# Convolutions, gate operands and gate diagonals issued earlier in a bidirectional hybrid layer

## The chip, the core and the metric

One Trainium2 chip, one of its cores. The metric is the device time of one execution in microseconds. The core has TensorE (PE in the profile, with its weight loads as PEld), VectorE (DVE), ScalarE (ACT), GpSimd (POOL) and SyncE (SP, which issues DMAs).

## The reference, cut to what matters

One layer on a sequence of 2048 tokens with 2048 channels, in float32:

```
mod = silu(c) @ w_ada + b_ada;  shift, scale, gate = split(mod)
h = rms_norm(x) * (1 + scale) + shift
u_pool, u_lru, g_pool, g_lru = split(h @ w_in + b_in)
y_pool = pool_mixer(u_pool)                  # centred means of 2, 4, 8, 16 tokens, then a 256x256 product
v = depthwise_conv(u_lru, width 4)
for both directions:
    r, i = sigmoid(v @ w_gate + b_gate)
    a = exp(-8 r softplus(-lambda));  b = sqrt(1 - a^2) * i * v
    h_dir = scan(h = a h + b)
y_lru = h_forward + h_backward
y = concat(rms_norm(y_pool) * silu(g_pool), rms_norm(y_lru) * silu(g_lru)) @ w_out + b_out
out = rms_norm(x + gate * y)
```

## The kernel before, in words

Every product in float32 is done as three matmuls over operands split into a high and a low part (`mm3`): high by high, high by low, low by high. The program is one loop over 352 steps `t`. A step is 24 matmuls of 128x512 that add one slice of the contraction to four banks of PSUM. Steps 0 to 127 make the plain part of the input projection, steps 128 to 239 the rest of it with seven products in place of eight, steps 240 to 351 the output projection in the same way. Each step needs a tile `m` (activations, split in L184 on ScalarE and L185 on VectorE, three buffers) and a tile `s` (weights). When the last slice of a bank is added, it is evacuated: in steps 128 to 239 by `in_evac` (L494 to L513), some on ScalarE, most on VectorE.

The mixers run beside that as background work. `at(t, fn)` appends a function to the list `bg[t]`, which is called at the end of step t, in the order of the list. An LRU unit is one head, one direction `d` and one block of 512 tokens, and starts at a step `b` (tables `L_AT`; mostly five steps apart). Its parts are: for the forward direction a depthwise convolution in place on `u` (L560 on ScalarE, then L562 three times on VectorE, for each of two channel tiles, accumulating in `cv`); `split`, which makes the gate operand `uch` in its two parts (L567 on ScalarE, L568 on VectorE); `gates`, two groups of 12 matmuls for each of two channel tiles; `sig` (L581, L583); `expo`, tanh and exponential (L589, L593); `scan`, which begins with a square root on ScalarE (L597), then products (L602, L603) and the scan itself (L608 forward, L612 backward). There is one buffer for `uch` and one for the gate weights `gw` (L537, L538). The first four units of each head run forward, the other four backward and are merged with them (L630 to L635).

Late in the program (steps 257 to 259) `gate_rows` makes the row vector of the adaLN gate: it builds diagonal matrices from columns (L771) in a buffer of the pool `raw`, and a float32 matmul with ones (L774) turns them into rows; L775 evacuates them. Near that stands the norm of the last block: a matmul, a square root (L422) and a reciprocal (L423).

A scheduler decides the order of the instructions on each engine: it goes by the order in which the program issues them as priority, and by its own estimate of when operands are there. So a function issued earlier gets a higher priority than what follows, on every engine it uses. On the chip each engine runs its list in that order. Buffers come from pools: `raw` has eight buffers for loads, evacuated gates, scan results and diagonals, `ps_m` six banks of PSUM and `px` two.

Of the kernel before, what the change touches and what calls it, by code (L numbers as in the profile page):

```python
# [11 lines left out]
ALU = mybir.AluOpType  # L12
# [33 lines left out]
def layer(ctx: ExitStack, tc: tile.TileContext, xc, xn, c, wada, win, wgate, wpool, wout, vecs, consts, bout, fng, out):  # L46
    nc = tc.nc
# [15 lines left out]
    def raw(name):  # L63
        return raw_p.tile([128, 2, TB], F32, tag="raw", name=name)
# [7 lines left out]
    def pm():  # L72
        return ps_m.tile([128, TB], F32, tag="pm", name="pm")

    def px():
        return ps_x.tile([128, TB], F32, tag="px", name="px")
# [15 lines left out]
    cst = one.tile([128, NC], F32, name="cst")  # L92
    ones = one.tile([128, 128], F32, name="ones")
# [4 lines left out]
    gcol = one.tile([128, 16], F32, name="gcol")  # L98
# [20 lines left out]
    bg = defaultdict(list)  # L119

    def at(t, fn, *a):
        bg[t].append((fn, a))
# [6 lines left out]
    def where1(t):  # L129

        g, i = divmod(t, 32)
        if g == 0 and i < 16:
            return 0, i % 2, i // 2
        return g, i // 8, i % 8
# [7 lines left out]
    def where2(t):  # L142

        sg, i = divmod(t - T1, SG)
        return sg, i // 8, i // 4 % 2, i % 4
# [17 lines left out]
    def m_load(t):  # L163
        if t >= NT:
            return
        r = raw("xr")
        if t < T1:
            g, tb, p = where1(t)
            load(out=r, in_=xc[tb, p] if g < 2 else xscr[tb][p])
        else:  # L170
            sg, k, q, p = where2(t)
            load(out=r, in_=moving("in" if sg < 2 else "out", PRODUCTS[k][1], p, q))
        xraw[t] = r
# [43 lines left out]
    def w_load(g, p):  # L217
        r = raw("wr")
        load(out=r, in_=win[g, p])
        wraw[g, p] = r  # L220
# [120 lines left out]
    def step(bk, sk, p, m, tiles, first, last, by_j=False, more=False):  # L341

        s = S_t[sk, p]
        for n, j in [(n, j) for j in range(2) for n in tiles] if by_j else [(n, j) for n in tiles for j in range(2)]:
            mm3(bk[n], s, slice(n * 128, (n + 1) * 128), m, j, first and j == 0, last and j == 1, more)
# [53 lines left out]
    def ada_load(i):  # L399
        t = big("ada")[:, :D]  # L400
        load(out=t, in_=wada[i])
        ada_t[i] = t
# [143 lines left out]
    def lru_unit(g, h, d, tb, b, last):  # L546
# [91 lines left out]
                del u_t[g]  # L638

        if d == 0:  # L640
            at(b, conv)
        at(b, split)
        at(b + 2, gates, 0)
        at(b + 3, sig, 0)
        at(b + 3, gates, 1)
# [107 lines left out]
    def rows_open():  # L753
# [9 lines left out]
        for i, (tb, kind) in enumerate([(2, "P"), (2, "L"), (3, "P"), (3, "L")]):  # L763
            act(out=fin["rn"][:, i], in_=rn_t[tb, kind], func=AF.Copy)
            rn_t[tb, kind] = fin["rn"][:, i]

    def gate_rows(i):
        t = raw("dg")[:, 0]
        for j in range(4):
            k = 4 * i + j  # L770
            nc.vector.tensor_scalar(out=t[:, j * 128:(j + 1) * 128], in0=cst[:, 0:128], scalar1=gcol[:, k:k + 1], scalar2=None,  # L771
                                    op0=ALU.mult)
        ps = px()
        nc.tensor.matmul(out=ps, lhsT=ones, rhs=t, start=True, stop=True)  # L774
        act(out=fin["gate"][:, i * TB:(i + 1) * TB], in_=ps, func=AF.Copy)  # L775
        if i == 3:
            vtt(out=fin["gb"], in0=fin["gb"], in1=fin["gate"], op=ALU.mult)
# [95 lines left out]
    for i in range(16):  # L873
        b = 17 + i * 5 // 4
# [32 lines left out]
    for g, bs in L_AT.items():  # L907
        h = GROUPS[g][1]
        for d in range(2):
            b = bs[4 * d]  # L910
# [9 lines left out]
    for i in range(32):  # L920
        p, k, q = i // 8, (0, 2, 1, 3)[i // 2 % 4], i % 2
# [4 lines left out]
    for sg in range(2):  # L926
        b = NT1 + SG * sg
# [47 lines left out]
    for t, tb, kind in rn_at:  # L975
        at(t, rn, tb, kind)
    at(256, rows_open)
    for i in range(4):
        at(257 + i * 3 // 4, gate_rows, i)


    unit_at = {T1 - 6 + 2 * u: u for u in range(112)}
# [10 lines left out]
    def s_step(p):  # L993
        ada_dot(16 + 2 * p)
        ada_dot(17 + 2 * p)
        scale_fin(p)
        w_split(0, p)
# [4 lines left out]
    for t in range(NT):  # L1002

        if t < 16:
            if t % 2 == 0:
                p = t // 2
                if p + 1 < 8:
                    w_load(0, p + 1)
                m_load(t + 2)
                m_load(t + 3)  # L1010
                if p + 2 < 8:
                    ada_load(16 + 2 * p + 4)
                    ada_load(16 + 2 * p + 5)
        if t >= 14:
            while loaded < t + AHEAD:
                loaded += 1
                m_load(loaded)
        if t < T1:
            g, tb, p = where1(t)
            key = (g, tb)  # L1020
            sk = g
            first, last = p == 0, p == 7
        else:
            sg, k, q, p = where2(t)
            more = k in CHAINED and (sg == 3 or sg == 2 and k == 6)
            key = (8 + sg, CHAINED[k] if more else k, q)
            sk = (8 + sg, PRODUCTS[k][0])
            first, last = p == 0 and not more, p == 3
        e = t + W_AHEAD - 25
        if 0 <= e < 96 and e % 32 < 8:  # L1030
            w_load(e // 32 + 1, e % 32)
        if t + W_AHEAD in unit_at:
            unit_load(unit_at[t + W_AHEAD])
        for o, i in late:
            store(out=o, in_=i)
        late.clear()

        if t < 14:
            if t % 2 == 0:
                s_step(t // 2 + 1)  # L1040
        if 32 <= t + 3 < 64:
            modulate(t + 3)
        m_split(t + 2)
        e = t - 25
        if 0 <= e < 96 and e % 32 < 8:
            w_split(e // 32 + 1, e % 32)
        if t in unit_at:
            unit_split(unit_at[t])

        if key not in banks:  # L1050
            if t == 0:
                banks[key] = [px(), px(), pm(), pm()]
            else:
                banks[key] = [px(), px(), pm(), pm()] if q and t >= T1 and (sg == 3 or sg == 2 and k > 1) else [pm() for _ in range(4)]
        bk = banks[key]
        if t < NT - 4:
            step(bk, sk, p, M_t.pop(t), range(4), first, last, t == 0, t >= T1 and more)
        if t < NT - 4 and (q if t >= T1 else tb == 3):
            del S_t[sk, p]
        if last:  # L1060
            if t < T1 or sg < 2 or k not in CHAINED.values() or sg == 2 and k == 0:
                del banks[key]
            if t < 32:
                evac_raw(g, tb, bk)
            elif t < T1:
                evac(g, tb, bk)
            elif t < NT1:
                in_evac(sg, k, q, bk)
            elif t < NT - 1:
                out_evac(sg - 2, k, q, bk, range(4))  # L1070
            else:
                for i in range(4):
                    for p_ in range(4):
                        step(bk, sk, p_, M_t[t - 3 + p_], (i,), False, p_ == 3, more=True)
                    last_fin(i, bk[i])
                    if i:
                        out_row(1, i - 1, 3, 2)
                out_row(1, 3, 3, 4)

        for u in units:  # L1080
            if u[0] == t:
                start_unit(u)
        for fn, a in bg.pop(t, ()):
            fn(*a)
# [65 lines left out]
```

## Time and profile before

| | |
|---|---|
| Time, median of 3 runs | 2210.78 us (2209.96 to 2211.48) |
| Profiled execution, its own time | 2209.89 us |
| Its span in the profile | 2207.8 us |
| Mean granted clock of TensorE | 0.994 |
| PE busy | 2165.6 us (98%) |
| DVE busy | 1800.6 us (82%) |
| ACT busy | 1248.7 us (57%) |

Matmuls are pipelined, so PE's busy time counts overlapping records; how fast PE works is read from the number of matmuls in an undisturbed stretch, and what is lost from the stretches where it waits or where the granted clock is below 1.00. Times in the rows are microseconds from the start of the span.

### The profile page before, as it was taken

Reading aid. Unit: us, or ns where it says so; the run is one execution under the profiler, and the core shown is the slowest. Engines: PE = TensorE matmul, PEld = TensorE weight load, DVE = VectorE, ACT = ScalarE, POOL = GpSimd, SP = SyncE. Lnnn points to the kernel's source line nnn. Section 1 sums busy time; section 2 is a strip of 40 time slices with the busy share of each in tenths; the row PEclk is TensorE's granted clock in tenths of the full one; section 3 lists DMA queues with packets and bytes.
Section 4 is the critical chain, followed back from the end, with each engine's and each line's share of the span. In section 5 each row is a group of like instructions: output and inputs, shape, how many; then the busy total and the mean of one; then the engine's idle time right before and its main releaser. Section 6 shows DMA issues by size and latency. Waiting matters only on the chain. (4 is left out here: it accounts for less than half of the span.)

```text
span 2207.8 us, 25720 instructions
## 1 busy us (share of the span) xinstructions
PE 2165.6 (98%) x9448; PEld 1776.3 (80%) x9448; DVE 1800.6 (82%) x2174; ACT 1248.7 (57%) x1548; POOL 6.2 (0%) x40
## 2 busy tenths in 40 slices
PE   7999999999999999999999999999999999999998
PEld 6888887888888888878778887877886888888886
DVE  7999766588986877877889777899888668976789
ACT  4555578577865676656665666653654333433233
POOL 0000000000000000000000000000000000000000
PEclk9999999999999999999999999999999999999999
DMA  9879945768787988886888887698778657897664
GB/s 390 338 276 334 334 150 200 244 209 309 287 313 292 334 335 298 306 310 218 292 290 295 288 305 275 213 331 311 247 263 315 237 191 241 327 331 262 208 237 175
DMA packets 161342, 613.22 MB, mean 278 GB/s; under 512 B 17856, under 2 KB 19136, under 8 KB 153280
## 3 DMA queue, kind: packets, MB, share of 16 engines
q1 hardware_dynamic: 154880, 588.51, 74.7%
q10 hardware_dynamic: 6336, 23.07, 2.7%
q8 instruction: 74, 1.21, 0.2%
q14 instruction: 52, 0.43, 0.1%
HBM read 467.85 MB, written 143.65 MB: 277 GB/s over the span
## 5 line engine op out<-in xcount | busy, mean ns | idle before, releaser
L338 PE MATMUL pm<-m,s 128*128 128x512 f32 x7764 | 1800.2, 391 | 6.3 <-DVE gr L504 4.6
L338 PEld LDWEIGHTS pm<-m,s 128*128 128x128 f32 x7764 | 1459.3, 188 | 320.1 <-issue 7.0
L184 ACT ACTIVATE m<-xr 128x1024 fp32r<-128x1024 f32 x350 | 368.9, 1055 | 470.6 <-PE pm L338 329.7
L185 DVE TENSOR_TENSOR m<-xr,m 128x1024 fp32r<-128x1024 f32 x350 | 426.0, 1218 | 128.1 <-ACT m L184 127.1
L338 PE MATMUL px<-uch,gw 128*128 128x512 f32 x768 | 190.6, 395 | 7.0 <-DVE uch L568 3.2
L338 PEld LDWEIGHTS px<-uch,gw 128*128 128x128 f32 x768 | 145.3, 190 | 41.5 <-DVE uch L568 5.5
L338 PE MATMUL px<-m,s 128*128 128x512 f32 x660 | 162.7, 392 | 13.2 <-ACT m L387 12.3
L331 ACT ACTIVATE s<-yr 128x1024 fp32r<-128x1024 f32 x104 | 109.5, 1053 | 103.4 <-DMA yr<-in_win_dram 24.0
L338 PEld LDWEIGHTS px<-m,s 128*128 128x128 f32 x660 | 124.1, 189 | 40.8 <-ACT m L387 12.3
L332 DVE TENSOR_TENSOR s<-yr,s 128x1024 fp32r<-128x1024 f32 x104 | 126.6, 1217 | 20.0 <-ACT s L331 19.9
L406 DVE CUSTOM_DVE_ANT_0 ada<-ada,cact 128x2048 f32<-128x2048 f32 x47 | 107.3, 2285 | 24.8 <-DMA ada<-in_wada_dram 24.8
L279 DVE TENSOR_TENSOR tr<-tr 128x1024 f32<-128x1024 f32 x64 | 78.0, 1218 | 26.9 <-DMA tr<-in_wout_dram 9.9
L602 DVE SCALAR_TENSOR_TENSOR th<-rg,th 128x512 f32<-128x512 f32 x64 | 42.4, 684 | 34.5 <-ACT th L597 34.4
L583 DVE TENSOR_TENSOR ig<-ig,u 128x512 f32<-128x512 f32 x64 | 43.9, 686 | 23.7 <-ACT ig L581 23.4
L567 ACT ACTIVATE uch<-u 128x512 fp32r<-128x512 f32 x64 | 38.2, 624 | 44.2 <-DVE u L562 44.1
L200 ACT ACTIVATE xr<-xr,shv 128x512 f32<-128x512 f32 x64 | 44.1, 718 | 27.0 <-DVE xr L199 27.0
L823 DVE TENSOR_TENSOR x<-x,gb 128x1024 f32<-128x1024 f32 x32 | 38.9, 1220 | 18.7 <-DMA x<-in_xn_dram 18.7
L581 ACT ACTIVATE ig<-px,vec 128x512 f32<-128x512 f32 x64 | 43.7, 683 | 15.7 <-PE px L338 15.4
L562 DVE SCALAR_TENSOR_TENSOR cv<-u,vec,cv 128x512 f32<-128x512 f32 x64 | 45.9, 742 | 6.8 <-ACT cv L560 6.7
L199 DVE SCALAR_TENSOR_TENSOR xr<-xr,sc,rl 128x512 f32<-128x512 f32 x64 | 45.3, 743 | 6.9 <-DMA xr<-in_xc_dram 6.9
L581 ACT ACTIVATE rg<-px,vec 128x512 f32<-128x512 f32 x64 | 43.9, 686 | 6.9 <-PE px L338 6.4
L338 PE MATMUL px<-uch,pw 128*128 128x512 f32 x192 | 47.5, 394 | 0.2 <-DVE uch L692 0.2
(194 smaller groups left out, 1703.0 us busy)
## 6 DMA issues: line engine op xcount, KB each, us to landing
xr<-xs SPq DMA_DIRECT2D x112, 512.0 KB, 5.9
ada<-in_wada_dram SPq DMA_DIRECT2D x47, 1024.0 KB, 7.9
yr<-in_win_dram SPq DMA_DIRECT2D x72, 512.0 KB, 5.7
yr<-ys SPq DMA_DIRECT2D x72, 512.0 KB, 4.6
xr<-h SPq DMA_DIRECT2D x64, 512.0 KB, 5.8
xr<-t SPq DMA_DIRECT2D x64, 512.0 KB, 4.8
xr<-in_xc_dram SPq DMA_DIRECT2D x63, 512.0 KB, 6.8
tr<-xs SPq DMA_DIRECT2D x48, 512.0 KB, 5.9
```

The costliest lines, as they stand in the source:

```text
L184: act(out=m[:, 0], in_=r, func=AF.Copy)
L185: vtt(out=m[:, 1], in0=r, in1=mf[:, 0], op=ALU.subtract)
L199: stt(out=r[:, j], in0=r[:, j], scalar=sc[:, k:k + 1], in1=rr, op0=ALU.mult, op1=ALU.mult)
L200: act(out=r[:, j], in_=r[:, j], func=AF.Identity, bias=shv[:, k:k + 1])
L279: vtt(out=a, in0=a, in1=b, op=ALU.subtract)
L331: act(out=s[:, 0], in_=r, func=AF.Copy)
L332: vtt(out=s[:, 1], in0=r, in1=s.bitcast(F32)[:, 0], op=ALU.subtract)
L338: nc.tensor.matmul(out=ps, lhsT=a[:, x, j, asl], rhs=b[:, y, j], start=first and i == 0, stop=last and i == 2, skip_group_check=more)
L406: nc.vector.tensor_tensor_reduce(out=t, in0=t, in1=cact["t"], op0=ALU.mult, op1=ALU.add, scale=1.0, scalar=0.0, accum_out=mod[:, i:i + 1])
L562: stt(out=a if k < 3 else U[i][:, us], in0=src, scalar=cw, in1=a, op0=ALU.mult, op1=ALU.add)
L581: act(out=v, in_=st.pop(("ps", w, i)), func=AF.Sigmoid, bias=V("b_gate", (d * 4 + h) * 4 + 2 * w + i))
L583: vtt(out=st["i", i], in0=st["i", i], in1=U[i][:, us], op=ALU.mult)
```

## The change

It has three parts. The convolution of a forward unit is appended to the list of the step before the unit's own (`b - 1`), where it comes behind the exponentials of the unit in front if that one started five steps earlier. `split` is put at the front of the list of step `b`, ahead of what stands there already: the square roots and scans of the unit in front, merges, the split of new gate weights. So that this works, a unit is set up one step earlier. And the diagonals are made in a function of their own, `gate_diag`, eight at steps 255 and 256, while the four `gate_rows` are left with matmul and evacuation, at steps 258, 258, 259 and 260 in place of 257, 257, 258 and 259.

```diff
--- before.py
+++ after.py
@@ -638,8 +638,8 @@
                 del u_t[g]
 
         if d == 0:
-            at(b, conv)
-        at(b, split)
+            at(b - 1, conv)
+        bg[b].insert(0, (split, ()))
         at(b + 2, gates, 0)
         at(b + 3, sig, 0)
         at(b + 3, gates, 1)
@@ -764,14 +764,19 @@
             act(out=fin["rn"][:, i], in_=rn_t[tb, kind], func=AF.Copy)
             rn_t[tb, kind] = fin["rn"][:, i]
 
+    dg = {}
+
+    def gate_diag(i):
+
+        t = dg[i] = raw("dg")
+        for j in range(8):
+            k = 8 * i + j
+            nc.vector.tensor_scalar(out=t[:, j // 4, j % 4 * 128:(j % 4 + 1) * 128], in0=cst[:, 0:128], scalar1=gcol[:, k:k + 1],
+                                    scalar2=None, op0=ALU.mult)
+
     def gate_rows(i):
-        t = raw("dg")[:, 0]
-        for j in range(4):
-            k = 4 * i + j
-            nc.vector.tensor_scalar(out=t[:, j * 128:(j + 1) * 128], in0=cst[:, 0:128], scalar1=gcol[:, k:k + 1], scalar2=None,
-                                    op0=ALU.mult)
         ps = px()
-        nc.tensor.matmul(out=ps, lhsT=ones, rhs=t, start=True, stop=True)
+        nc.tensor.matmul(out=ps, lhsT=ones, rhs=dg[i // 2][:, i % 2], start=True, stop=True)
         act(out=fin["gate"][:, i * TB:(i + 1) * TB], in_=ps, func=AF.Copy)
         if i == 3:
             vtt(out=fin["gb"], in0=fin["gb"], in1=fin["gate"], op=ALU.mult)
@@ -975,8 +980,10 @@
     for t, tb, kind in rn_at:
         at(t, rn, tb, kind)
     at(256, rows_open)
+    for i in range(2):
+        at(255 + i, gate_diag, i)
     for i in range(4):
-        at(257 + i * 3 // 4, gate_rows, i)
+        at(258 + i * 3 // 4, gate_rows, i)
 
 
     unit_at = {T1 - 6 + 2 * u: u for u in range(112)}
@@ -1078,7 +1085,7 @@
                 out_row(1, 3, 3, 4)
 
         for u in units:
-            if u[0] == t:
+            if u[0] - 1 == t:
                 start_unit(u)
         for fn, a in bg.pop(t, ()):
             fn(*a)
```

In the rows that follow, an engine's instructions stand in their order: line, operation, tiles written and read, shape, and how often in a row. VectorE around the unit of step 57, before (`th`, `ig`, `rg`, `hf` and `carry` are of the unit in front, `u_925` and `u_928` the two channel tiles of the head):

```order
L185 TENSOR_TENSOR m<-xr,m 128x1024
L260 TENSOR_TENSOR s<-wr,s 128x1024
L602 SCALAR_TENSOR_TENSOR th<-rg,th 128x512 x2
L603 TENSOR_TENSOR ig<-ig,th 128x512 x2
L608 SCALAR_TENSOR_TENSOR hf<-rg,carry,ig 128x512 x2
L616 COPY carry<-hf 128x1
L562 SCALAR_TENSOR_TENSOR cv<-u_925,vec,cv 128x512
L616 COPY carry<-hf 128x1
L562 SCALAR_TENSOR_TENSOR cv<-u_928,vec,cv 128x512
L562 SCALAR_TENSOR_TENSOR cv<-u_925,vec,cv 128x512
L562 SCALAR_TENSOR_TENSOR cv<-u_928,vec,cv 128x512
L562 SCALAR_TENSOR_TENSOR u_925<-u_925,vec,cv 128x512
```

And after the change:

```order
L562 SCALAR_TENSOR_TENSOR cv<-u_925,vec,cv 128x512
L562 SCALAR_TENSOR_TENSOR cv<-u_928,vec,cv 128x512
L562 SCALAR_TENSOR_TENSOR cv<-u_925,vec,cv 128x512
L562 SCALAR_TENSOR_TENSOR cv<-u_928,vec,cv 128x512
L562 SCALAR_TENSOR_TENSOR u_925<-u_925,vec,cv 128x512
L562 SCALAR_TENSOR_TENSOR u_928<-u_928,vec,cv 128x512
L185 TENSOR_TENSOR m<-xr,m 128x1024
L260 TENSOR_TENSOR s<-wr,s 128x1024
L568 TENSOR_TENSOR uch<-u_925,uch 128x512
L568 TENSOR_TENSOR uch<-u_928,uch 128x512
L602 SCALAR_TENSOR_TENSOR th<-rg,th 128x512 x2
L603 TENSOR_TENSOR ig<-ig,th 128x512 x2
```

The convolution (L562) and the split (L568) have moved ahead of the products and scans of the unit in front (L602 to L616); the tile `m` (L185) that stood ahead of the products now stands between the convolution and the split.

VectorE around the reciprocal of the last norm and the first gate diagonals, before:

```order
L792 TENSOR_TENSOR o<-pm,o 128x512
L185 TENSOR_TENSOR m<-xr,m 128x1024
L322 TENSOR_TENSOR yr<-yr 128x1024
L423 RECIPROCAL sqP<-sqP 128x512
L323 TENSOR_TENSOR yc<-yr 128x1024
L185 TENSOR_TENSOR m<-xr,m 128x1024
L332 TENSOR_TENSOR s<-yc,s 128x1024
L332 TENSOR_TENSOR s<-yr,s 128x1024
L771 TENSOR_SCALAR dg<-cst,gcol 128x128 x8
```

And after the change, where the lines behind the diff are higher by three to five (the diagonals are L774):

```order
L797 TENSOR_TENSOR o<-pm,o 128x512
L774 TENSOR_SCALAR dg<-cst,gcol 128x128 x8
L423 RECIPROCAL sqP<-sqP 128x512
L185 TENSOR_TENSOR m<-xr,m 128x1024
L322 TENSOR_TENSOR yr<-yr 128x1024
L185 TENSOR_TENSOR m<-xr,m 128x1024
L323 TENSOR_TENSOR yc<-yr 128x1024
L774 TENSOR_SCALAR dg<-cst,gcol 128x128 x7
L332 TENSOR_TENSOR s<-yc,s 128x1024
```

The first eight diagonals have moved from behind the reciprocal to ahead of it, and the tile `m` that stood three rows ahead of the diagonals, and ahead of the reciprocal, now stands behind both.

VectorE around the evacuation of step 139 (L496), before, with the convolution of the unit of step 139 (`u_5263`, `u_5266`) beside the scans of the one in front:

```order
L602 SCALAR_TENSOR_TENSOR th<-rg,th 128x512
L562 SCALAR_TENSOR_TENSOR cv<-u_5263,vec,cv 128x512
L608 SCALAR_TENSOR_TENSOR hf<-rg,carry,ig 128x512
L603 TENSOR_TENSOR ig<-ig,th 128x512
L616 COPY carry<-hf 128x1
L562 SCALAR_TENSOR_TENSOR cv<-u_5263,vec,cv 128x512
L608 SCALAR_TENSOR_TENSOR hf<-rg,carry,ig 128x512
L185 TENSOR_TENSOR m<-xr,m 128x1024
L616 COPY carry<-hf 128x1
L496 SCALAR_TENSOR_TENSOR u_6643<-pm,vec,u_6643 128x512
L496 SCALAR_TENSOR_TENSOR u_6646<-pm,vec,u_6646 128x512
L496 SCALAR_TENSOR_TENSOR u_6649<-pm,vec,u_6649 128x512
```

And after the change:

```order
L562 SCALAR_TENSOR_TENSOR cv<-u_5263,vec,cv 128x512
L603 TENSOR_TENSOR ig<-ig,th 128x512
L562 SCALAR_TENSOR_TENSOR cv<-u_5263,vec,cv 128x512
L562 SCALAR_TENSOR_TENSOR cv<-u_5266,vec,cv 128x512
L562 SCALAR_TENSOR_TENSOR u_5263<-u_5263,vec,cv 128x512
L608 SCALAR_TENSOR_TENSOR hf<-rg,carry,ig 128x512 x2
L616 COPY carry<-hf 128x1
L562 SCALAR_TENSOR_TENSOR cv<-u_5266,vec,cv 128x512
L616 COPY carry<-hf 128x1
L185 TENSOR_TENSOR m<-xr,m 128x1024
L562 SCALAR_TENSOR_TENSOR u_5266<-u_5266,vec,cv 128x512
L496 SCALAR_TENSOR_TENSOR u_6643<-pm,vec,u_6643 128x512
```

Six steps of the convolution stand ahead of the first L496 in place of two; the rest of the rows ahead of it are the same.

## Rows read from the trace of the kernel before

**Rows 1.** Busy time and share of the span by engine, instructions (page).

```profile
PE 2165.6 (98%) x9448; PEld 1776.3 (80%) x9448; DVE 1800.6 (82%) x2174; ACT 1248.7 (57%) x1548; POOL 6.2 (0%) x40
```

**Rows 2.** Timeline of PE, 922 to 952: start, length, work, [idle before <- releaser].

```profile
921.82 19.66 PE L338 MATMUL pm<-m,s 128*128 128x512 f32 x86
...
944.31 4.65 PE L338 MATMUL px<-uch,gw 128*128 128x512 f32 x11 [1.95 <-DVE uch L568]
```

**Rows 3.** PE's waits: total us, times, longest.

```profile
PE px L774 <- DVE dg L771: 4.8, 1, 4.8
PE pm L338 <- DVE gr L504: 4.6, 2, 2.4
PE px L338 <- DVE uch L568: 3.2, 3, 2.0
PE px L338 <- ACT uch L567: 3.0, 3, 2.1
PE pm L338 <- DVE u L498: 1.6, 1, 1.6
PE px L338 <- ACT rg L581: 0.7, 1, 0.7
```

**Rows 4.** Stretches: length, busy PE, PEld, DVE, ACT, POOL, granted clock, DMA.

```profile
360.00:364.00 4.00, 3.24 (x7) 2.22 (x8) 4.00 (x6) 3.87 (x5) 0.00 (x0) 0.59 0.75 237
...
600.00:615.00 15.00, 13.93 (x62) 11.12 (x61) 15.00 (x18) 13.56 (x18) 0.00 (x0) 1.00 0.86 317
...
942.00:950.00 8.00, 5.94 (x18) 4.08 (x19) 7.49 (x8) 3.31 (x4) 0.00 (x0) 0.79 0.76 257
...
1465.00:1480.00 15.00, 15.00 (x66) 11.89 (x65) 14.58 (x22) 7.19 (x9) 0.00 (x0) 1.00 0.97 348
...
1680.00:1685.00 5.00, 4.42 (x6) 2.18 (x7) 2.45 (x8) 1.19 (x2) 0.00 (x0) 0.50 1.01 409
```

**Rows 5.** Timeline of PE, 340 to 366.

```profile
341.90 16.71 PE L338 MATMUL pm<-m,s 128*128 128x512 f32 x73
360.76 1.22 PE L338 MATMUL px<-uch,gw 128*128 128x512 f32 x2 [2.15 <-ACT uch L567]
361.90 1.65 PE L338 MATMUL pm<-m,s 128*128 128x512 f32 x3
363.35 2.83 PE L338 MATMUL px<-uch,gw 128*128 128x512 f32 x10
```

**Rows 6.** Timeline of VectorE, 340 to 366.

```profile
348.87 1.23 DVE L185 TENSOR_TENSOR m<-xr,m 128x1024 fp32r<-128x1024 f32 x1 [5.36 <-ACT m L184]
...
359.31 1.40 DVE L562 SCALAR_TENSOR_TENSOR u<-u,vec,cv 128x512 f32<-128x512 f32 x2
```

**Rows 7.** Timeline of VectorE, 922 to 952.

```profile
927.50 1.23 DVE L322 TENSOR_TENSOR yr<-yr 128x1024 f32<-128x1024 f32 x1 [1.50 <-DMA yr<-in_win_dram]
...
943.57 0.68 DVE L568 TENSOR_TENSOR uch<-u,uch 128x512 fp32r<-128x512 f32 x1
```

**Rows 8.** Timeline of PE, 1660 to 1704.

```profile
1662.54 13.29 PE L338 MATMUL pm<-m,s 128*128 128x512 f32 x54
1680.59 3.78 PE L774 MATMUL px<-dg,ones 128*128 128x512 f32 x4 [4.76 <-DVE dg L771]
```

**Rows 9.** Timeline of VectorE, 1660 to 1704.

```profile
1669.57 1.22 DVE L185 TENSOR_TENSOR m<-xr,m 128x1024 fp32r<-128x1024 f32 x1
...
1671.84 3.34 DVE L423 RECIPROCAL sqP<-sqP 128x512 f32<-128x512 f32 x1
...
1679.66 1.65 DVE L771 TENSOR_SCALAR dg<-cst,gcol 128x128 f32<-128x128 f32 x8
```

**Rows 10.** Costliest groups of instructions (page): busy, mean ns of one, idle before, releaser.

```profile
L567 ACT ACTIVATE uch<-u 128x512 fp32r<-128x512 f32 x64 | 38.2, 624 | 44.2 <-DVE u L562 44.1
```

**Rows 11.** Timeline of VectorE, 880 to 902.

```profile
890.13 0.69 DVE L602 SCALAR_TENSOR_TENSOR th<-rg,th 128x512 f32<-128x512 f32 x1 [5.11 <-ACT th L597]
...
898.74 2.06 DVE L496 SCALAR_TENSOR_TENSOR u<-pm,vec,u 128x512 f32<-128x512 f32 x3
```

## The prediction

> **What bounds the kernel now.** I read the page's busy shares first, then PE's waits, then the timeline of each engine around every long wait, then the granted clock there. PE is busy for 98% of the span [rows 1], and where nothing disturbs it 86 matmuls take 19.66 us, 0.229 us each [rows 2]. The change leaves their number alone, so it can only act on the stretches where PE doesn't run at that pace. There are two kinds. One is waits [rows 3]: 4.8 us in one for the gate diagonals (dg), 4.6 us in two for the evacuation L504, 3.2 and 3.0 us for the two halves of a unit's gate operand (L568 on VectorE, L567 on ScalarE), 1.6 us for the evacuation L498, 0.7 us for a sigmoid. The other is half clock: the granted clock has a mean of 0.59, 0.79 and 0.50 in three stretches that follow such waits [rows 4], that is 1.2 GHz instead of 2.4 for part or all of them; after the 0.79 stretch began, 11 matmuls took 4.65 us, 0.42 each [rows 2]. The reader is to see that the disturbed places are few, and that most of them wait for just what the diff moves.
>
> **What the change does, place by place.** It adds no arithmetic: the same convolutions, splits, diagonals and matmuls are issued, two activation-table loads fewer. So every term below is a wait at one place, before and after, with the half clock that belongs to it. Names A to I are mine.
>
> A, the unit of step 57. From 358.61 (341.90 + 16.71) to 366.18 (363.35 + 2.83) PE does 2 + 3 + 10 matmuls [rows 5]; at 0.229 these are 3.4 us, and they take 7.57: 4.1 us are lost, 2.15 of it the wait for L567, the rest mostly half clock. VectorE had stood idle for 5.36 us before 348.87 [rows 6], and did the convolution only after the scans, its last two steps at 359.31. In the new order the six convolution steps (0.70 each by the 359.31 row, so 4.2 us) and both splits stand ahead of the previous unit's products and scans, and fall into that idle time. The operand is then there some 5 us before PE's turn. Late next is the tile m that now stands behind the scans: they end no later than the convolution and scans together did, about 358, and PE reaches that tile around 361, its matmuls at 361.90 being the next of their kind [rows 5]. Gain 4.1; lowest 2 if that tile comes a little late and the half clock goes anyway.
>
> D, the unit of step 144. PE leaves the plain matmuls at 941.48 (921.82 + 19.66), and up to 944.31 it does one matmul: 2.83 - 0.23 = 2.6 lost; the 11 that follow cost 4.65 - 11 x 0.229 = 2.1 more at half clock [rows 2]: 4.7. VectorE finishes the first split only at 943.57, and it idled 1.50 us for a DMA ahead of 927.50 [rows 7]. Six convolution steps (4.2) and two splits (1.2) moved ahead of the products and scans end around 936, some 5 us before PE's turn. Gain 4.7, lowest 2.6.
>
> B, the unit of step 92. VectorE is busy for 15.00 of 15 us and PE for 13.93 [rows 4]; the wait for L568 in it is what D leaves of the 3.2 [rows 3], about 1.2. With no idle time to fill, work moved forward pushes other work back, so what is gained for the operand can be lost at a tile m. I take 0.8, between -0.5 and 1.2.
>
> E, the unit of step 172: the wait of 0.7 for L581 [rows 3] is a sigmoid that comes late after a late operand. I take 0.5, between 0 and 0.7.
>
> F, the gate rows. PE waits 4.76 us at 1680.59 [rows 8], since the first eight diagonals begin on VectorE only at 1679.66, behind a reciprocal of 3.34 us [rows 9]; then it works 4.42 us at clock 0.50 [rows 4], of which half, 2.2, is lost. Together 7.0. In the new order the diagonals stand ahead of the reciprocal and the gate rows a step later, so neither is left. But eight diagonals (1.65) and the reciprocal (3.34) now stand ahead of the tile m of step 258, which before began at 1669.57 [rows 9]: it ends at about 1669.57 + 1.6 + 3.3 + 1.2 = 1675.7. PE wants it after 48 of the 54 matmuls that begin at 1662.54 (13.29 us) [rows 8], at 1674.35. A new wait of about 1.3. The two diagonal tiles also hold two of the eight buffers of the raw pool until their matmuls are done, which delays the load of a tile two steps on, and the evacuation of the gate rows behind it on ScalarE. I find no row of such a wait; it lies between 0 and 2.4, PE's longest for an evacuation [rows 3], and I take 1.1. So F gains 7.0 - 1.3 - 1.1 = 4.6, between 3.3 and 5.7.
>
> G, the wait of 1.6 for L498 [rows 3]. Both split copies on ScalarE (0.62 each) [rows 10] now stand ahead of the square roots that VectorE's products wait for, while the splits on VectorE leave the stretch ahead of L498. I take 0.6 more wait, between 0 and 1.2.
>
> H, around step 140. L496 begins at 898.74 [rows 11] and frees the banks of which PE needs the first soon after; PE doesn't wait there now. In the new order four more convolution steps (2.8) stand ahead of it, against VectorE's 5.11 us of idle time before 890.13 [rows 11], of which I think about 1 us goes, because a split on ScalarE, twice as wide as the copies of [rows 10], moves behind the exponentials. I take a new wait of 0.5, between 0 and 1.7.
>
> I, steps 222 to 228. Of L504's two waits one is not touched by the order, the other (2.2 in all) becomes some 0.7 shorter; behind it one more m tile (1.22, the length of that in [rows 9]) stands ahead of a pool weight that PE needs. I take 0.5 lost, between -0.7 and 1.2.
>
> Sum: 4.1 + 4.7 + 0.8 + 0.5 + 4.6 - 0.6 - 0.5 - 0.5 = 13.1. The profiled execution took 2209.89, so 2196.8; the median of the runs is 0.89 above it: **2198**. With every term at its better end the gain is 17, with every term at its worse end about 3.
>
> **Rivals.** First, the half clock follows new waits too. It followed the waits at 360, 944 and 1680, and yet the waits of 2.2 near 1464 left the clock at 1.00 up to 1480 [rows 4]. If the waits that F, H and G leave (1.3, 0.5, 2.2) were each followed by a stretch as at A, which cost 4.1 - 2.15 = about 1.9, the gain falls to 7.4: 2203. The Trainium skill, "TensorE: Matmul & The Clock Gate", section "Part 1: The HAM clock gate", says that the slow clock is the default and activity releases it. By that rule the 2203 is what any real gap costs; the trace agrees at three waits and not at 1464.
>
> Second, VectorE's work is the bound, and the wait only changes its name. For it speak the full VectorE at B [rows 4] and the 82% of the whole [rows 1]; against it the 5.36 and 1.50 us of idle time that A and D have in front [rows 6, 7]. Then PE waits for tiles m in A, B, D and E as long as now, and F less G, H and I gives 3.0: 2208, no change that can be told (a measurement of this kernel tells some 0.2%, 4.4 us, from nothing).
>
> Third, on the other side: the evacuations of PSUM lose their place. At H four more convolution steps come ahead of L496. If there was no idle time behind it, this is a wait of 2.7 and a half clock of 1.9, 4.6 at one place. The eight forward units of steps 128 to 202 all have evacuations close by. Three such places eat the 13.1, from four on the kernel is slower by more than 0.2%; with five it is 2221. Against it: before the change the same VectorE work stood there in nearly the same number, and it is one step that the convolution moves.
>
> Last, that nothing moves where it matters: the order shows otherwise at A, D and F.
>
> **How the numbers follow.** The forecast 0.60, by itself 2191 to 2203; the clock rival 0.16; VectorE as the bound 0.14; the evacuations 0.10. The range leaves out the evacuation case and a tenth at the low end: 2190 to 2208. Faster by over 0.2% (below 2206.4): the forecast, the clock rival, a fifth of the third case: 0.79. Within: 0.11. Slower: 0.10.
>
> **What would show it.** Right: PE's waits for L567, L568 and dg gone but for fragments, the granted clock at 1.00 around 360, 944 and 1680, the idle 5.36 us of VectorE near 349 filled by L562. A new wait for L185 of a microsecond or so in the step of the gate rows would confirm F's term. Wrong: waits for L185 near 350, 595 or 950 (the second rival), waits for L496, L498 or L500 longer than 2 us between 870 and 1330 (the third), or clock 0.5 behind a wait of a microsecond (the first).

## The result, and the profile after

The changed kernel takes 2196.28 us (median of 6 runs, 2191.28 to 2201.53) beside 2210.76 for the kernel before (6 runs): a ratio of 0.993, 95% interval 0.9915 to 0.9945. The forecast was 2198, faster; the range was 2190 to 2208. The six runs of the changed kernel lie 10 us apart, so single profiles of it are read for their places and not for their totals. The profiled execution took 2198.52 us, its span is 2196.5.

PE's busy share after, to be held against [rows 1]:

```profile
PE 2159.8 (98%) x9448; PEld 1775.8 (81%) x9448; DVE 1801.0 (82%) x2174; ACT 1243.8 (57%) x1546; POOL 6.2 (0%) x40
```

As many instructions on PE and VectorE as before, two fewer on ScalarE (the table loads). PE's waits after, as in [rows 3] (total us, times, longest):

```profile
...
PE pm L338 <- DVE u L498: 3.4, 1, 3.4
PE px L338 <- ACT rg L581: 3.0, 1, 3.0
PE pm L338 <- DVE m L185: 2.0, 2, 1.1
PE px L338 <- ACT gate L780: 2.0, 1, 2.0
PE pm L338 <- DVE gr L504: 1.4, 1, 1.4
...
PE pm L338 <- DVE u L496: 0.6, 1, 0.6
```

The waits for L567, L568 and dg are gone, 11 us in all. New ones stand in their place: L185 (1.06 us near 1120 and 0.94 us at 1668), the gate row's evacuation (L780), and a sigmoid (L581) near 610. That sigmoid is another than the 0.7 us of [rows 3]: the old wait stood at 1143 and is gone. The wait for L498 has doubled. The stretches that answer to [rows 4] (length, busy time of PE, PEld, DVE, ACT, POOL, granted clock, DMA share, GB/s):

```profile
357.00:361.00 4.00, 4.00 (x19) 3.29 (x19) 4.00 (x5) 1.92 (x4) 0.00 (x0) 1.00 0.98 311
597.00:612.00 15.00, 11.96 (x53) 9.55 (x52) 15.00 (x18) 9.79 (x13) 0.14 (x2) 1.00 0.93 330
937.00:945.00 8.00, 8.00 (x37) 6.63 (x36) 7.35 (x10) 2.85 (x4) 0.00 (x0) 1.00 0.89 304
1319.00:1326.00 7.00, 6.18 (x16) 4.94 (x17) 5.96 (x8) 0.66 (x1) 0.00 (x0) 0.55 0.85 291
```

Full clock and a full PE at the places that were disturbed before, near 357 and 937; half clock in one place that had none, behind the longer wait for L498 at 1319; and a PE busy for only 11.96 of 15 us at 597, beside a VectorE busy for all of them.

Where the time came from can be read by the start of one and the same matmul in both traces. The matmuls are counted from the first; the fourth column is after less before, at the ends of the stretches in which it changes:

```
matmul   before     after    difference   what lies between
  1488    353.92    353.88      0.0       A begins
  1536    368.96    364.78     -4.2       A
  2568    604.88    599.36     -5.5       B, the operand
  2616    615.85    613.64     -2.2       B, the sigmoid
  3600    839.60    836.93     -2.7
  3888    905.00    903.14     -1.9       H
  4056    947.86    941.27     -6.6       D
  4704   1099.35   1090.14     -9.2       L504 near 1090
  4848   1132.01   1124.16     -7.9       a tile m near 1120
  4896   1145.01   1135.41     -9.6       E
  5712   1332.64   1327.03     -5.6       G
  6288   1465.88   1457.76     -8.1       I
  7152   1666.66   1659.04     -7.6
  7200   1685.97   1671.54    -14.4       F, the diagonals
  7344   1719.68   1708.29    -11.4       F, what it gives back
```

At A the timeline of PE, as in [rows 5], has no gap left:

```profile
337.79 19.89 PE L338 MATMUL pm<-m,s 128*128 128x512 f32 x87
357.52 2.89 PE L338 MATMUL px<-uch,gw 128*128 128x512 f32 x12
360.25 4.02 PE L338 MATMUL pm<-m,s 128*128 128x512 f32 x17
```

And VectorE, as in [rows 6], does the convolution from 342.82, where it had been idle:

```profile
342.82 2.79 DVE L562 SCALAR_TENSOR_TENSOR cv<-u,vec,cv 128x512 f32<-128x512 f32 x4 [2.58 <-ACT cv L560]
...
349.12 1.29 DVE L568 TENSOR_TENSOR uch<-u,uch 128x512 fp32r<-128x512 f32 x2
...
355.15 1.21 DVE L185 TENSOR_TENSOR m<-xr,m 128x1024 fp32r<-128x1024 f32 x1
```

The operand is complete at 350.4, seven microseconds before PE begins with it at 357.52. The tile m behind the scans is there at 356.4, and PE wants it at 360.25.

At the gate rows (F), PE, as in [rows 8]:

```profile
1668.00 5.51 PE L338 MATMUL pm<-m,s 128*128 128x512 f32 x23 [0.94 <-DVE m L185]
1673.35 1.88 PE L779 MATMUL px<-dg,ones 128*128 128x512 f32 x4
...
1684.94 1.65 PE L338 MATMUL px<-m,s 128*128 128x512 f32 x6 [1.98 <-ACT gate L780]
```

VectorE there, as in [rows 9]:

```profile
1661.96 1.65 DVE L774 TENSOR_SCALAR dg<-cst,gcol 128x128 f32<-128x128 f32 x8
1663.53 3.34 DVE L423 RECIPROCAL sqP<-sqP 128x512 f32<-128x512 f32 x1
1666.79 1.16 DVE L185 TENSOR_TENSOR m<-xr,m 128x1024 fp32r<-128x1024 f32 x1
```

And ScalarE:

```profile
1683.34 1.06 ACT L184 ACTIVATE m<-xr 128x1024 fp32r<-128x1024 f32 x1 [2.33 <-DMA xr<-t]
1684.31 0.58 ACT L780 ACTIVATE gate<-px 128x512 f32<-128x512 f32 x1
```

The diagonals wait for nothing, and the tile m stands behind the reciprocal as the order said: 0.94 us lost. The evacuation of a gate row at 1684.31 waits on ScalarE behind the split of a tile (L184), and that waits for the DMA that brings the tile. PE, which needs the bank, loses 1.98. The DMA is late because its issue was. SyncE holds the load of the tile ahead (L172) back until VectorE is done with an older tile; it goes out at 1675.22, and the load in question behind it, at 1676.58. SyncE's longest wait from 1662 to 1690 (total us, times, longest):

```profile
SPq L172 <- DVE m L185: 12.5, 2, 8.1
```

### The profile page after: what moved, and what is told of

Read it like the earlier page. It is cut to its first block, busy times and chain, and to the rows that moved or that the text cites. A ratio compares the mean times of both kernels' runs of the same rounds, so it can differ in the third digit from the quotient of the medians.

```text
span 2196.5 us, 25702 instructions
## 1 busy us (share of the span) xinstructions
PE 2159.8 (98%) x9448; PEld 1775.8 (81%) x9448; DVE 1801.0 (82%) x2174; ACT 1243.8 (57%) x1546; POOL 6.2 (0%) x40
## 4 chain that ended last, share of the span: by engine, by line
PE 63%; DVE 17%; DMA 10%; issue 4%; ACT 4%; SPq 0%; DVEq 0%; ACTq 0%
PE pm L338 51%; PE px L338 12%; DVE m L185 3%; DMA yr<-in_win_dram 2%; DVE th L612 1%; DMA yr<-ys 1%; DMA xr<-h 1%; DMA gl<-gs 1%; DVE th L602 1%; DVE s L332 1%; DVE cv L562 1%; DVE tr L279 1%; DMA tr<-xs 1%; DVE ig L603 1%; DMA ys<-gl 1%
## 5 line engine op out<-in xcount | busy, mean ns | idle before, releaser
L184 ACT ACTIVATE m<-xr 128x1024 fp32r<-128x1024 f32 x350 | 369.0, 1055 | 458.9 <-PE pm L338 321.7
L185 DVE TENSOR_TENSOR m<-xr,m 128x1024 fp32r<-128x1024 f32 x350 | 426.8, 1220 | 102.9 <-ACT m L184 101.2
L338 PE MATMUL px<-uch,gw 128*128 128x512 f32 x768 | 186.0, 390 | 3.0 <-ACT rg L581 3.0
L331 ACT ACTIVATE s<-yr 128x1024 fp32r<-128x1024 f32 x104 | 109.6, 1054 | 108.8 <-DMA yr<-in_win_dram 26.6
L279 DVE TENSOR_TENSOR tr<-tr 128x1024 f32<-128x1024 f32 x64 | 78.2, 1222 | 34.8 <-DMA tr<-xs 17.0
L562 DVE SCALAR_TENSOR_TENSOR cv<-u,vec,cv 128x512 f32<-128x512 f32 x64 | 45.1, 749 | 25.6 <-ACT cv L560 25.5
L602 DVE SCALAR_TENSOR_TENSOR th<-rg,th 128x512 f32<-128x512 f32 x64 | 42.0, 688 | 14.8 <-ACT th L597 14.8
L581 ACT ACTIVATE ig<-px,vec 128x512 f32<-128x512 f32 x64 | 43.7, 683 | 15.4 <-PE px L338 15.3
L568 DVE TENSOR_TENSOR uch<-u,uch 128x512 fp32r<-128x512 f32 x64 | 41.9, 687 | 11.2 <-ACT uch L567 11.2
L581 ACT ACTIVATE rg<-px,vec 128x512 f32<-128x512 f32 x64 | 44.0, 687 | 11.9 <-PE px L338 11.5
```

What stands on the lines that cost most here:

```text
L184: act(out=m[:, 0], in_=r, func=AF.Copy)
L185: vtt(out=m[:, 1], in0=r, in1=mf[:, 0], op=ALU.subtract)
L279: vtt(out=a, in0=a, in1=b, op=ALU.subtract)
L331: act(out=s[:, 0], in_=r, func=AF.Copy)
L338: nc.tensor.matmul(out=ps, lhsT=a[:, x, j, asl], rhs=b[:, y, j], start=first and i == 0, stop=last and i == 2, skip_group_check=more)
L562: stt(out=a if k < 3 else U[i][:, us], in0=src, scalar=cw, in1=a, op0=ALU.mult, op1=ALU.add)
```

## The experiments

**The diagonals alone.** `gate_diag` and the shortened `gate_rows` as in the change, forward and backward units as before:

```diff
+    for i in range(2):
+        at(255 + i, gate_diag, i)
     for i in range(4):
-        at(257 + i * 3 // 4, gate_rows, i)
+        at(258 + i * 3 // 4, gate_rows, i)
```

> Only the gate diagonals are made two steps ahead; convolution and split stand as before. Theory (three separate parts, each worth what its own places show): the wait for the diagonals (4.8 us) and its half clock go, a wait of about 1 us for the tile m behind the reciprocal and one of about 2 us for the evacuated gate row come in their place; all other waits stay. Some 4 us faster than before, about 2207. Rival (the two new waits at the gate rows come only because PE arrives there earlier by what the convolutions gained): they are absent here, and the gain is 6 to 7 us, about 2204.

Measured: 2210.42 beside 2214.19, a ratio of 0.9988 (0.9975 to 1.0001): at most a few microseconds, perhaps nothing. One of its waits:

```profile
PE px L338 <- ACT gate L780: 2.9, 2, 2.1
```

So the wait for the evacuated gate row shows though PE has gained nothing ahead of it, and for this wait the rival falls. The wait for a tile m at the reciprocal does not show: the one wait for L185 in this profile, 0.4 us, is at 362. For that wait the rival is not refuted. The same matmuls as above: from 6360 to 7200 this kernel gains 8.3 us, up to 7344 it gives back 5.8 (waits for L780 and a half clock at 1697.6). The net gain there is 2.5 us, less than the expected 4.

**The split of the backward units alone.** The units are set up one step earlier, as in the change:

```diff
         if d == 0:
             at(b, conv)
-        at(b, split)
+            at(b, split)
+        else:
+            bg[b].insert(0, (split, ()))
```

> Only the split of the backward units moves to the front of its step; forward units and diagonals as before. Theory (near 1320 the two split copies and the split of the gate weights, now ahead of the square roots on ScalarE, make the scans and with them L498 late): the wait for L498 grows from 1.6 to about 3.5 us, and the kernel is the same or 1 to 3 us slower, 2211 to 2214. Rival (that wait grew because PE came there 10 us earlier, and VectorE could not follow): it stays at 1.6, and the kernel is within 1 us of before.

Measured: 2209.98 beside 2214.19, 0.9984 (0.9972 to 0.9996).

```profile
PE pm L338 <- DVE u L498: 1.7, 1, 1.7
```

The wait for L498 doesn't grow in this profile, and the kernel is a little faster, not slower, so the theory falls. The rival had the wait right, but by the ratio the kernel is some 3.5 us faster than before, not within 1; what gives this is not shown.

**The change without that part.** Its counterpart: the changed kernel with `at(b, split)` for d = 1.

> The changed kernel with the split of the backward units back at the end of its step; convolution and split of the forward units and the diagonals as changed. Theory (the split of the unit of step 202 costs the 3.4 us wait for L498 and the half clock behind it): the wait is 1.6 or less and the half clock is gone, 3 to 4 us faster than the changed kernel there, less up to 2 us that the same edit may have brought near step 225: 2193 to 2195. Rival (PE comes too early for VectorE): the wait stays above 3 us, time 2196 or more.

Measured: 2198.53, 0.9932 (0.9914 to 0.995); the changed kernel itself had 0.9914 beside it. Two of its waits:

```profile
PE pm L338 <- DVE gr L504: 5.0, 2, 2.8
...
PE pm L338 <- DVE u L498: 0.9, 1, 0.9
```

L498 is short, as the theory wanted, but the next run shows that this says nothing, and the time did not fall.

**The changed kernel, a second and a third time.**

> The changed kernel unchanged, for a second profile of it. If the waits and the half clock are set by the order of the instructions, the same places show again: 3.0 us for L581 near 610, 3.4 us for L498 near 1320, 2.0 us for L780 near 1685, about 1 us twice for L185. If they are chance, they move. Time 2196, as the six runs of it.

> The changed kernel once more, beside the other two on the same chip, for its time there and a third profile. Theory (which of the waits for L581, L498 and L504 show depends on when the DMAs of an execution land, not on the order alone): the waits before 1000 and at the gate rows (L780, 2 us or more) show again, those for L498 and L504 differ from both earlier profiles by 1 us or more. Time 2193 to 2197.

Measured: 2193.48, 0.9914 (0.9897 to 0.9931), and 2198.53, 0.9928 (0.9912 to 0.9944). The waits of the second profile:

```profile
PE px L338 <- ACT gate L780: 3.0, 2, 2.1
PE px L338 <- ACT rg L581: 1.6, 1, 1.6
...
PE pm L338 <- DVE u L498: 0.5, 1, 0.5
```

In the third L581 costs 3.6, L498 2.2, L504 1.9, L780 3.1. So A, D, H and L780 come back each time. L498 (3.4, 0.5, 2.2), L504 (1.4, none, 1.9), L581 (3.0, 1.6, 3.6) and the tile m at the reciprocal (0.94, none, 0.3) do not keep their size, though VectorE has its 2174 instructions in one and the same order in all three. For L498 the two first traces show what differs. ScalarE, first profile, near 1301:

```profile
1301.22 1.06 ACT L184 ACTIVATE m<-xr 128x1024 fp32r<-128x1024 f32 x1 [3.01 <-DMA xr<-h]
1302.19 0.67 ACT L581 ACTIVATE rg<-px,vec 128x512 f32<-128x512 f32 x1
```

ScalarE, second profile, the same split:

```profile
1295.39 1.06 ACT L184 ACTIVATE m<-xr 128x1024 fp32r<-128x1024 f32 x1 [1.92 <-DMA xr<-h]
```

The sigmoids of the unit in front stand behind the split of a tile m, and that waits for its DMA. PE is 3.0 us further on in the second trace (it begins the 84 matmuls ahead of the wait at 1294.26, against 1297.24), ScalarE 5.8 us: the DMA came 2.9 us earlier in relation to PE, and that much shorter is the wait for L498, at the end of the chain sigmoid, exponential, square root, scan, L498.

For L581 it is a transfer too, 40 us ahead. VectorE near 570 in the first, second and third profile in turn (L279 combines two loaded tiles):

```profile
570.46 1.23 DVE L279 TENSOR_TENSOR tr<-tr 128x1024 f32<-128x1024 f32 x1 [1.16 <-DMA tr<-xs]
```

```profile
568.87 1.22 DVE L279 TENSOR_TENSOR tr<-tr 128x1024 f32<-128x1024 f32 x1
```

```profile
570.87 1.23 DVE L279 TENSOR_TENSOR tr<-tr 128x1024 f32<-128x1024 f32 x1 [2.07 <-DMA tr<-xs]
```

From there to L581 VectorE has no idle time, so what it lost at 570 it still lacks at 605: 1.16, nothing and 2.07 us there, 3.0, 1.6 and 3.6 for L581. In every kernel here with the forward units moved and the products of the adaLN rows in place, L581 costs 1.5 to 1.6 where L279 doesn't wait and 2.9 to 3.6 where it does.

**The diagonals one step later, then in another buffer.** In the first, `at(256 + i, gate_diag, i)`; in the second also:

```diff
-        load(out=fin["fg"], in_=fng.broadcast_to([128, D]))
...
-        t = dg[i] = raw("dg")
+        t = dg[i] = fin["fg"][:, i * 1024:(i + 1) * 1024].rearrange("p (a b) -> p a b", a=2)
...
+    def fg_load():
+        load(out=fin["fg"], in_=fng.broadcast_to([128, D]))
+
+    at(262, fg_load)
```

> The changed kernel with both groups of eight diagonals made one step later, still in buffers of the raw pool. In its order the tile m of step 258 stands ahead of the reciprocal again, and the diagonals behind it. Theory: the wait of about 1 us for L185 at the reciprocal goes; the waits for the evacuated gate rows (L780, 2 to 3 us) stay, since the diagonals hold the same buffers. 1 us faster than the changed kernel, 2192 to 2196. Rival (the diagonals are now late): a wait for dg of 1 us or more.

> As the kernel with the diagonals one step later, and they are made in the row buffer of the final norm's gain, whose load moves behind the last gate row; so they hold no buffer of the raw pool. Theory (the waits for L780 come from the raw pool: the load of a tile waits for a buffer, its split on ScalarE waits for the load, and the evacuation stands behind the split): they vanish, 2 to 4 us better than with the diagonals one step later, 2190 to 2193. Rival (the evacuation is late by ScalarE's order alone, or the load by the DMA queue): the waits for L780 stay at 2 us or more, and the time with them.

Measured: 2193.05, 0.9914 (0.9898 to 0.993), and 2194.1, 0.9913 (0.9894 to 0.9931). One step later there is no wait for L185 at the reciprocal (but the second profile of the changed kernel has none either), none for dg comes, and L780 stays with 1.9. In the row buffer there is no wait for the evacuation (L779 in that file). Its PE behind that evacuation:

```profile
1681.36 3.33 PE L338 MATMUL px<-m,s 128*128 128x512 f32 x12
```

And its ScalarE, where the splits wait for PE and no more for the tile's DMA:

```profile
1681.10 1.06 ACT L184 ACTIVATE m<-xr 128x1024 fp32r<-128x1024 f32 x1 [0.39 <-PE pm L338]
```

SyncE's wait from 1662 to 1690, which at the longest is 8.1 us in the changed kernel and 8.5 with the diagonals one step later, is here:

```profile
SPq L172 <- DVE m L185: 1.8, 2, 1.1
```

So the theory's chain shows: the load is issued without the long hold, the split doesn't wait for it, and PE doesn't wait for the evacuation. These are single profiles, and the same wait was 0.8 in one kernel that kept the raw pool (the split put back, below). From matmul 7152 to 7344 the first gains 3.5 us on the kernel before, the second 6.5 (from -6.9 to -13.3). But the second pays just ahead of that stretch. Its diagonals need no buffer of the pool, and six of them now stand on VectorE ahead of a tile m and of the evacuation L796:

```profile
1655.31 1.26 DVE L773 TENSOR_SCALAR fg<-cst,gcol 128x128 f32<-128x128 f32 x6
```

PE waits 1.9 us for that evacuation at 1658.36, with half clock behind it:

```profile
PE pm L338 <- DVE sum L796: 1.9, 1, 1.9
```

Counted from matmul 7140, ahead of this wait, the gains are 2.6 and 3.9. The total, 2194.1, is above what was expected, and in it the two cannot be told apart: the second also lost at L581, 3.0 with a half clock behind it.

**The split back at the end of its step.** `at(b, split)` for all units in place of the insertion at the front.

> The changed kernel with split back at the end of its step's list, for all units; the convolution of the forward units stays a step earlier, the diagonals as changed. Theory (the convolution is the longer part, 4.2 us on VectorE against 1.3 for the split, and PE's waits near 360 and 944 are gone with it alone, the operand coming some 3 us later than in the changed kernel but still in time): no wait for L567 or L568 above 0.5 us, time 2195 to 2199. Rival (the split has to come ahead of the scans too): the waits for L567 and L568 near 360 and 944 are back with 1 to 2 us each and the half clock, 2202 to 2206.

Measured: 2195.04, 0.9927 (0.9907 to 0.9947).

```profile
PE px L338 <- DVE uch L568: 0.3, 1, 0.3
```

There is no wait for L567. The convolution's step is what counts; the front of the list is not needed for the waits near 360 and 944. At H the wait for L496 is 1.7 in this profile, against 0.5 to 0.6 with the split in front.

**The products of the adaLN rows four steps later.**

```diff
-        at(95 + 2 * i, ada_load, 32 + i)
-        at(96 + 2 * i, ada_dot, 32 + i)
+        at(99 + 2 * i, ada_load, 32 + i)
+        at(100 + 2 * i, ada_dot, 32 + i)
```

> The changed kernel with the loads and products of the adaLN gate rows (L406, 2.29 us each on VectorE) four steps later, so that the first stands behind L718 and not ahead of L715 near 603. Theory (the wait of 1.6 to 3.0 us for L581 near 610 is a chain: L406 ahead of L715 on VectorE, L716 behind it on ScalarE, L581 behind that): the wait is below 0.7 us, the kernel 1 to 3 us faster than the changed one up to there. Rival (VectorE is full from 585 to 616, and something else is late there in its place): a wait of 1 us or more for another line within 20 us of it.

Measured: 2195.79, 0.9928 (0.9911 to 0.9944). The chain in the changed kernel, VectorE:

```profile
602.63 2.29 DVE L406 CUSTOM_DVE_ANT_0 ada<-ada,cact 128x2048 f32<-128x2048 f32 x1
...
604.84 1.42 DVE L715 SCALAR_TENSOR_TENSOR gl<-py,vec,gl 128x512 f32<-128x512 f32 x2
```

And ScalarE behind it:

```profile
605.63 1.35 ACT L716 ACTIVATE py<-py 128x512 f32<-128x512 f32 x2 [3.10 <-DVE gl L715]
...
607.56 1.28 ACT L581 ACT_TABLE_LOAD   x1
608.86 0.69 ACT L581 ACTIVATE rg<-px,vec 128x512 f32<-128x512 f32 x1
```

The sigmoid that empties the bank for PE stands behind L716, that behind L715, and that behind a product of 2.29 us. With the products later the wait is 0.7 us, and no other stands within 20 us. At matmul 2616 this kernel is 4.6 us ahead of before, the changed one 2.2, 3.8 and 0.3 in its three profiles. Fair to hold beside it is the 3.8, for in this profile too L279 near 570 doesn't wait. So the product's place in the list costs about 0.8 us, and what L581 costs beyond 1.6 comes with the transfer. The theory holds for the chain, not for its whole size; the total moved no more than its interval.

**The forward units alone.** Convolution and split of d = 0 as changed, units set up one step earlier, all else as before.

> The kernel before with convolution and split of the forward units moved as in the change; backward units and diagonals as before. Theory (the forward units near 360 and 944 carry most of the gain): PE's waits for L567 and L568 are gone, the one for the diagonals (about 5 us) stays, and the kernel is 8 to 11 us faster than before. Rival (VectorE takes the gain back in the full stretches behind, so that it only shows together with the other parts): less than 5 us faster.

Measured: 2197.14 beside 2213.41, 0.9928 (0.9915 to 0.994): as much as the whole change in the same runs (0.9928). That is more than expected, and the wait for the diagonals, which nothing here moves, is shorter than before:

```profile
PE px L776 <- DVE dg L773: 1.8, 1, 1.8
```

VectorE of this kernel, the last idle time before it reaches the diagonals at 1665.69:

```profile
1648.57 1.29 DVE L305 TENSOR_TENSOR yr<-yr,sqL 128x512 f32<-128x512 f32 x2 [0.23 <-DMA yr<-ys]
```

And of the kernel before, where it reaches them at 1679.66:

```profile
1662.54 1.29 DVE L305 TENSOR_TENSOR yr<-yr,sqL 128x512 f32<-128x512 f32 x2 [2.13 <-DMA yr<-ys]
```

From there to the diagonals it takes 17.1 us in both. PE ends the matmuls ahead of the wait 16.3 us after this row here (1654.70 + 10.13) and 13.3 us before (1662.54 + 13.29): VectorE has caught up 3.0 us on PE, 1.9 of it by not waiting for this transfer, and the wait is 3.0 us shorter. From matmul 7152 to 7344 this kernel gains 5.6 us on the kernel before, with the old gate rows; the changed kernel gains 3.8, 2.5 and 1.9 in its three profiles, with the new ones.

**Both places mended.** The changed kernel with the diagonals in the row buffer, one step later, and the products four steps later.

> The changed kernel with two edits that each took a wait away alone: the diagonals one step later in the row buffer of the final norm's gain, and the products of the adaLN gate rows (L406) four steps later. Theory (both waits are separate): no wait for L780, none above 0.8 us for L581; 2 to 5 us faster than the changed kernel, 2188 to 2193. Rival (evacuations behind a full VectorE take up what PE gains): the waits for L498 and L504 together grow to 4 us or more and the time is that of the changed kernel, 2193 to 2197.

Measured: 2189.53 (5 runs, 2188.39 to 2191.04) beside 2198.53 for the changed kernel and 2213.41 for the one before; 0.9896 (0.9882 to 0.991). It beats both, by more than the expected 2 to 5 us beside these six runs of the changed kernel, whose median was 2193 to 2196 in others. Its waits:

```profile
PE pm L338 <- DVE u L498: 1.9, 1, 1.9
...
PE pm L338 <- DVE sum L796: 1.3, 1, 1.3
PE px L338 <- ACT gate L779: 1.1, 1, 1.1
PE px L338 <- ACT rg L581: 0.8, 1, 0.8
```

L581 is as expected, in a profile in which L279 near 570 doesn't wait. L796 stands behind six diagonals here too. The gate row's evacuation (L779 in this file) still costs 1.1, so that part of the expectation missed; on ScalarE it stands behind a split (L331) that waits 5.63 us for another DMA:

```profile
1674.94 1.06 ACT L331 ACTIVATE s<-yr 128x1024 fp32r<-128x1024 f32 x1 [5.63 <-DMA yr<-ss]
```

The waits for L498 and L504 did not grow: 2.3 together.

## Why the prediction was right, step by step

**A and D held to the tenth of a microsecond.** A was put at 4.1 and gave 4.1 to 4.2 in each of the three profiles (matmuls 1488 to 1536); D at 4.7 and gave 4.7 (3888 to 4056). The half clock went with the wait both times. The forward units alone carry the whole measured gain, 16.3 us, which the two terms, 8.8 us, explain to a good half. Of the rest their profile shows 5.6 at the gate rows and 2.4 near 1090, neither of which the forecast gave to them.

**H was right** (0.5 forecast, 0.8 lost, a wait of 0.6 for L496), and the order's warning at F, a wait of 1.3 for L185, came out as 0.94 in the first profile, but as nothing and 0.3 in the others.

**F was mis-sized.** Its 4.6 came out as 3.8 in the first profile (matmuls 7152 to 7344) and as 2.5 and 1.9 in the others; alone the part is worth 2.7 us by its ratio, and the interval of that takes in no change. The step of the forecast that was wrong here took the whole of the 4.76 us wait and the half clock behind it as what the diagonals cost. With the diagonals where they were, the wait is 4.8 before, 3.6 with the backward split moved and 1.8 with the forward units moved, there without a half clock. Of the 3.0 us between the first and the last, 1.9 are a transfer that landed late in the one and not in the other. The other unknown, the evacuation of the gate rows, had been put at 1.1 and costs 2.0 to 3.1. Its cause was given there without a row. The diagonals' buffers of the raw pool are now seen to be behind it, by SyncE's hold of 8.1 us in the changed kernel and 1.1 in the one with the row buffer, whose profile has no wait for the evacuation. Another transfer brought 1.1 of it back in the last kernel.

**B had the wrong sign:** 0.8 gained was forecast, and 2.0, 0.5 and 4.1 were lost in the three profiles (matmuls 1536 to 2616), though the operand itself came 1.3 earlier. I had looked for the wait that comes next at a tile m; it came at a sigmoid, behind a product of 2.29 us on a full VectorE. That was the second rival, true at this place. The 0.5, at the edge of the range given for B, is what the order costs; the rest of the 2.0 and 4.1 came with the late transfer near 570, which the full VectorE carries on, and with the half clock in the third.

**G, I and the wait near 1090** were read as set by the order. They are not by the order alone: with the order unchanged L498 took 3.4, 0.5 and 2.2 us. The wrong step for G was to take the 1.6 of one profile for a constant, and to add 0.6 of ScalarE's copies to it. Near 1090 the order of the chain that leads to L504 is the same before and after, and I counted nothing. The forecast named three stretches of half clock; the trace before has a fourth, here:

```profile
1090.00:1095.00 5.00, 4.67 (x13) 3.72 (x14) 5.00 (x8) 2.86 (x5) 0.00 (x0) 0.66 0.63 202
```

After, the wait fell from 2.4 to 1.4 and the half clock behind it was absent: 2.6 gained. I gave 2.1 instead of losing 0.5. These errors in the first profile, -2.8 at B, -3.7 at G, -0.8 at F, +2.6 and +2.6 at 1090 and I, nearly cancel. So the total is better than its terms, and that is luck: the mechanism was right at A, D and H, and the nearness of 2198 to 2196 doesn't prove the other terms.

**The rivals.** The clock: before, half clock shows in four stretches between the start and the end; in the three profiles of the changed kernel it shows in one, one and two. It followed the new wait of 3.4 for L498 in the first, that of 2.1 for L780 in the second and third, and that of 3.6 for L581 in the third. It did not follow the 3.0 for L581 nor the 2.0 for L780 in the first. The Trainium skill's page "TensorE: Matmul & The Clock Gate", section "Part 1: The HAM clock gate", has the slow clock as the default that activity releases; the traces agree with that in kind, and a wait of one size comes with and without the slow clock. VectorE as the bound was true at B and, as a tile m 1.1 us late near 1120, at E. The evacuations behind the convolution (third rival) cost a wait of 0.5 to 0.6 at H. The sign named for it, a wait for L498 above 2 us, did come (3.4 and 2.2 near 1320), but VectorE does no convolution in the 25 us ahead of it.

What stays open: how much each late transfer makes of the way from 2191 to 2200 us. The places are named (L581 near 610, L498 near 1320, L504 near 1082 and 1460), and for the first two the chain and its transfer; what lets a DMA land 1 to 3 us later in one execution was not tried. Ten profiles have the forward units moved: the four in which L279 near 570 waits for its transfer have spans of 2194.5 us and more, the six others 2193.3 and less. This speaks for L581 as the largest, but only argues it. The same is to be said of the last kernel's five runs, which lie within 2.7 us, where the changed kernel's lie 8 to 10 apart. Against it stands that the kernel with the products later alone has one run of 2202.25 beside five within 2 us.

## What to carry to other kernels

Where an engine that paces nothing has idle time just ahead of a chain that the pacing engine will wait for, move the chain's free part into that idle time: the price can be read from the stretch to a tenth of a microsecond. Where that engine is full, look along its list and along the lists of the engines behind it for what stands ahead of the next thing wanted; an unrelated product of 2.29 us cost PE some 0.8. Where that engine has no idle time, a late transfer at one place is still missing 40 us later. Before a wait of one profile goes into a sum, take a second profile of the same kernel: here the waits behind a DMA varied by 2 to 3 us between executions, and the gains at A and D by less than 0.1.

## What the hardware showed that was not expected

The gains of the parts seem not to add up: the forward units alone gave 0.9928, the whole change 0.9914 to 0.993, the two other parts 0.9988 and 0.9984 by themselves. The intervals, some 0.0012 to 0.0018 to either side, leave room for a part of that. And a wait of about 3 us for L581 was followed by half clock in three kernels (2.9 in the variant with the backward split put back, 3.0 in the one with the diagonals in the row buffer, 3.6 in the third profile of the changed one) but not in the first profile of the changed kernel.
